# Norm weights as 8 rows spread by TensorE, and the first block's products in another order

## The chip, the cores and the metric

The program runs on one core of one Trainium2 chip. The core has five engines that run their own instruction streams and wait for each other by semaphores: TensorE (in the profile PE, with its weight loads as PEld), VectorE (DVE), ScalarE (ACT), GpSimd (POOL) and SyncE (SP), which here only starts transfers; 16 DMA engines move data between device memory (DRAM), the on-chip buffer and, through the engines, the accumulators (PSUM). The time is the device time of one execution in microseconds (us). Before the change it was 972.03 us, the median of three runs (970.86 to 972.68).

## The reference

One layer of an inference step for a streaming encoder, on 1024 new prompt rows and 64 sample rows of 1024 features, all in f32. What matters here is the beginning:

```python
def rms_norm(x, w):
    xf = x.astype(jnp.float32)
    ms = jnp.mean(xf * xf, axis=-1, keepdims=True)
    return (xf * lax.rsqrt(ms + EPS)).astype(x.dtype) * w

h = rms_norm(x, norm_w) @ w_in          # x: 1088 rows x 1024, w_in: 1024 x 6144
sb_q, sb_k, sb_v, sb_z, cb_q, cb_k, cb_v, cb_z, g_sb, g_cb = jnp.split(h, SPLIT_POINTS, axis=-1)
...                                     # stick-breaking attention, chunk-band attention, gates,
...                                     # two projections, a merge, w_out and the residual
```

So every row is scaled by its own rsqrt and every feature by `norm_w` before any product with `w_in` can be formed.

## The kernel before

The order of the instructions on every engine is the order in which the code emits them (there is no scheduler); each engine works its list off in that order, and the tiles' buffers bring the waits.

**Split products.** Every f32 operand is taken apart into a rounded high part and the rest: `whi` is `wraw` rounded (ScalarE), `wlo` is `wraw` less `whi` (line 124); for the second 512 rows of the weights the tiles are called `wrawx`, `whix`, `wlox`. The same is done to the normed rows: `xa` and `xm` hold the high part of features 0 to 511 and 512 to 1023, `xm` (another half of that tile) and `xb` the low part. A product is then the sum of three: high by high, low by high, high by low, each a matmul with 128 rows as the stationary operand and 256 columns of `w_in` moving.

**Row tiles and blocks.** The 1088 rows are 9 tiles: the sample's 64 rows are tile 8 and come first, then tiles 0 to 7 of 128 rows (`TO = [8] + list(range(8))`). `w_in` is taken in blocks; the first eight (`nb = 8`) have 256 columns each and are the loop `for i in range(nb)`, with the nine tiles inside. A tile takes 24 products (8 slices of 128 features, 3 products each); tile 8 takes 16, since its high and low parts lie side by side in `xs`.

**Preparing a tile** goes along with block 0 and has three steps. `prep_s(t)`: ScalarE squares and sums the tile's rows (`sq`, line 261), GpSimd makes `rs`, the inverse root (lines 251 and 252). `prep_a(t)`: VectorE forms `xn`, the rows by `rs` by `nw`, in two halves (line 269). `prep_b(t)`: TensorE transposes `xn` in two times four pieces into PSUM (`pt`, line 280), ScalarE rounds each half out of it (`xs` line 283, `xa` and `xm` line 288), VectorE subtracts for the low part (lines 284 and 289). `nw` is `norm_w` on all 128 partitions, one transfer of 128 x 1024 values on SP's queue, second behind the sample's rows:

```python
load_x(8)
nw = p1.tile([128, D], F32, name="nw", bufs=1)
SP.dma_start(nw, norm_w[0:1, :].to_broadcast([128, D]))
load_x(0)
load_nat(0, 0)
load_nat(0, 1)
```

`W.split((0, 0), V)` and `W.split((0, 1))` take the first block's weights apart: `whi`, then `wlo` on VectorE, `whix`, then `wlox` on GpSimd. In block 0 the transposes of a tile stand a whole tile ahead of its products: those of tile 0 inside tile 8's products, those of tile 1 behind tile 8, those of tile t+2 behind tile t. Finished tiles are copied out of PSUM by `evac_nat` (`fl`, `vst`, lines 295 to 312) and stored by SP.

After the eight blocks come column units of another form, then both attentions with the remaining products laid among them, the two projections and the output product. TensorE's work in all of these is named in the profile by its line (673, 842, 948, 990, 1097, 1150, 1189, 1509).

Of the kernel before, what the change touches and what calls it, by code (L numbers as in the profile page):

```python
# [32 lines left out]
def hybrid_step_kernel(ctx: ExitStack, tc: tile.TileContext, x_prompt, x_sample, c_sbk, c_sbv, c_cbk, c_cbv,  # L33
# [109 lines left out]
    def xk(s, k):  # L143
        return xhl[s][k // 4][:, k % 4]
# [56 lines left out]
    with ExitStack() as ph:  # L201
# [13 lines left out]
        def load_x(t):  # L215
            xt = p1.tile([128, D], F32, name="xt", bufs=4)
            SP.dma_start(xt[:rows(t)], tok(x_prompt, x_sample, t))
            xts[t] = xt
# [4 lines left out]
                   [128, 4, 256], "" if h == 0 else "x")  # L223

        load_x(8)
        nw = p1.tile([128, D], F32, name="nw", bufs=1)
        SP.dma_start(nw, norm_w[0:1, :].to_broadcast([128, D]))
        load_x(0)
        load_nat(0, 0)
        load_nat(0, 1)  # L230
# [25 lines left out]
        def prep_s(t):  # L256
            r = rows(t)
            sq = p1.tile([128, D], F32, name="sq", bufs=1)
            ms = p1.tile([128, 1], F32, name="ms", bufs=4)
            rst[t] = p1.tile([128, 1], F32, name="rs", bufs=4)  # L260
            A.activation(sq[:r], xts[t][:r], AF.Square, accum_out=ms[:r])
            rsqrt(rst[t][:r], ms[:r], 1.0 / D, 1)

        def prep_a(t):
            r = rows(t)
            xt = xts.pop(t)
            xn = p1.tile([128, D], F32, name="xn", bufs=2)
            for c in (slice(0, 512), slice(512, D)):
                V.scalar_tensor_tensor(xn[:r, c], xt[:r, c], rst[t][:r], nw[:r, c], op0=OP.mult, op1=OP.mult)
            xns[t] = xn  # L270
# [169 lines left out]
                load_raw(2 * i + 4)  # L440

        load_x(3)
        prep_s(8)
        prep_a(8)
        prep_s(0)
        prep_b(8)
        prep_a(0)
        W.split((0, 0), V)
        W.split((0, 1))
        prep_s(1)  # L450
        load_x(4)
        pend, raw1 = [], None
        for i in range(nb):
            for ti, t in enumerate(TO):
                r = rows(t)
                last = (i, ti) >= (nb - 1, NT - 3)
                ps = (psA if ti % 3 == 2 and not last else psF).tile([128, 512], F32, name="acc")[:, :256]
                ns = 2 if t == 8 else 3
                steps = [(k, n) for k in range(KT) for n in range(ns)]
                if i == 0 and ti < 2:  # L460
                    steps.sort(key=lambda e: (e[1], e[0]))
                for m, (k, n) in enumerate(steps):
                    if i == 0 and ti == 0 and m == 4:
                        prep_b(0)
                    w = W.sp[i, k // 4][n // (ns - 1)][:, k % 4]
                    x = xs[:, k] if t == 8 else xk(n % 2, k)[:, xc(t):xc(t) + r]
                    TE.matmul(ps, x, w, start=m == 0, stop=m == len(steps) - 1)  # L467
                if i == 0 and ti == 0:
                    prep_a(1)
                    prep_s(2)  # L470
                    load_x(5)
                if len(pend) >= 3 or (pend and pend[0][0] < i and ti > 3):
                    post_nat(*pend.pop(0))
                if i == 0 and ti + 2 < NT:
                    if ti + 3 < NT:
                        prep_a(TO[ti + 3])
                    prep_b(TO[ti + 2])
                    if ti + 7 < NT:
                        load_x(TO[ti + 7])
                    if ti + 4 < NT:  # L480
                        prep_s(TO[ti + 4])
                got = evac_nat(i, t, ps)
                if raw1:
                    norm_nat(*raw1)
                    pend.append(raw1[:3])
                raw1 = (i, t) + got if got else None
                if i == 0:
                    if ti == 2:
                        load_nat(1, 0)
                        load_nat(1, 1)  # L490
                        SP.dma_start(wqk[:, 0], q_norm_w[0:1, :].to_broadcast([128, 64]))
                        SP.dma_start(wqk[:, 1], k_norm_w[0:1, :].to_broadcast([128, 64]))
                if ti in (3, 6) and i > 0 or ti in (5, 6) and i == 0:
                    h = 1 if ti == 6 else 0
                    if i + 1 < nb:
                        W.split((i + 1, h))
                    if i + 2 < nb:
                        load_nat(i + 2, h)
                    elif h == 0:
                        load_raw(i + 2 - nb)  # L500
                if (i, ti) == (4, 2):
                    load_rb()
                if 0 <= 9 * i + ti - 40 < 8:
                    make_rb(9 * i + ti - 40)
                if i >= 5 and p1x is not None and not pend and not raw1 and ti >= 3:
                    p1x.close()
                    p1x = None
                    tp = sx.enter_context(tc.tile_pool(name="tp", bufs=1))
                    pad(tp, 64)
                    tms = [[tp.tile([128, 4, HF], F32R, name=f"t{n}{s}") for s in "hl"] for n in range(4)]  # L510
                    ws = sx.enter_context(tc.tile_pool(name="ws", bufs=3))
                    tq = ph.enter_context(tc.tile_pool(name="tq", bufs=3))
                    tjobs = iter(make_t(tms, tq))
                    tw = [3]
                if p1x is None:
                    tw[0] -= 1
                    if tw[0] < 0:
                        next(tjobs, None)
                if (i, ti) == (nb - 1, 5):
                    prep(0)  # L520
                if (i, ti) == (nb - 1, 6):
                    presum(1)
                if (i, ti) == (nb - 1, 7):
                    prep(1)
                if (i, ti) in ((0, 4), (2, 3)):
                    cache_load("sb" if i == 0 else "cb")
                at = {(1, 1): 0, (1, 4): 1, (1, 7): 2, (2, 1): 3}
                if (i, ti) in at:
                    cache_pair("sb", at[i, ti])
                if (i - 2, ti) in at:  # L530
                    cache_pair("cb", at[i - 2, ti])
                if (i, ti) in ((1, 1), (1, 5)):
                    for s in range(2):
                        h = ti // 4
                        for c in range(2):
                            o = 512 + c * HF
                            G.tensor_copy(xhl[s][h][:, :, o:o + 32],
                                          xs[:, 4 * h:4 * h + 4, 64 * s + 32 * c:64 * s + 32 * c + 32])
                if (i, ti) == (1, 0):
                    V.tensor_scalar(wqk[:, 0], wqk[:, 0], -0.125, None, op0=OP.mult)  # L540
# [1054 lines left out]
```

## Time and profile before

| what | value |
|---|---|
| median of 3 runs | 972.03 us |
| profiled execution, its own time | 971.06 us |
| its span, first to last instruction | 969.3 us |
| HBM read and written | 112.94 MB and 62.00 MB |
| SP's queue (q1) | 159.98 MB, 56.2% of 16 DMA engines |
| ScalarE's queue (q10) | 8.33 MB, 2.7% |
| loads of `xt` from the prompt, 512 KB each | 5.2 us from issue to landing (median of 8) |
| loads of `wraw` from `w_in`, 512 KB each | 4.4 us (median of 31) |

A line of the timeline reads: start and duration in us, engine, line of the code, operation, what is written from what, shape, and in brackets how long the engine sat idle before it and who ended that. In a line of groups the busy time, the mean in ns and the idle time stand behind the count. In a row of stretches the limits come first, then the length, then busy time and instructions of PE, PEld, DVE, ACT and POOL, the clock, the share of the DMA engines and GB/s. A busy TensorE need not be a fast one: a matmul's duration is modelled and overlaps the next, so the pace is read from weight loads and from the distance between starts.

### The profile page before, as it was taken

How to read it: one execution, taken by the hardware profiler on the slowest of the kernel's cores; microseconds unless marked ns; L12 is line 12 of the kernel's file. 1: busy time of each engine (PE TensorE's matmuls, PEld its weight loads, DVE VectorE, ACT ScalarE, POOL GpSimd, SP SyncE). 2: the span in 40 equal slices, each digit the busy share in tenths (PEclk: the TensorE clock that was granted, in tenths of full speed). 3: DMA queues.
4: the chain of work that ended last, by engine and by line, in shares of the span. 5: the costliest groups of instructions: out<-in, count | busy, mean ns of one | idle time of the engine just before them, and what ended most of it. 6: DMA issues, size and time to landing. Idle time of an engine off the chain costs nothing.

```text
span 969.3 us, 20419 instructions
## 1 busy us (share of the span) xinstructions
PE 951.8 (98%) x7604; PEld 906.1 (93%) x7604; DVE 587.9 (61%) x1166; ACT 475.5 (49%) x1056; POOL 393.6 (41%) x391
## 2 busy tenths in 40 slices
PE   6999999999999999999999999999999999999998
PEld 5999999999999999999999987777888988999998
DVE  5456665696454555543332298776777865499735
ACT  6544443344444343333332377667886874465220
POOL 3276664215454566655542200011331111586641
PEclk9999999999999999999999999999999999999999
DMA  7727567534646565555533997769799832862742
GB/s 243 226 84 244 196 223 253 177 93 133 183 138 191 182 182 176 154 178 168 164 96 92 271 251 216 181 173 246 226 292 255 245 105 82 260 193 70 221 133 78
DMA packets 173512, 176.28 MB, mean 182 GB/s; under 512 B 30753, under 2 KB 157597, under 8 KB 173286
## 3 DMA queue, kind: packets, MB, share of 16 engines
q1 hardware_dynamic: 161878, 159.98, 56.2%
q10 hardware_dynamic: 8720, 8.33, 2.7%
q0 software_dynamic: 2816, 6.69, 2.2%
q8 instruction: 60, 0.98, 0.5%
q14 instruction: 38, 0.31, 0.1%
HBM read 112.94 MB, written 62.00 MB: 180 GB/s over the span
## 4 chain that ended last, share of the span: by engine, by line
PE 95%; ACT 1%; DMA 1%; SPq 1%; issue 0%; POOL 0%; DVE 0%; ACTq 0%; DVEq 0%
PE b L673 30%; PE acc L467 20%; PE b L1509 8%; PE z L1097 7%; PE o L1189 7%; PE pt L1150 7%; PE b L990 5%; PE acc L842 5%; PE acc L948 4%; PE pk L352 1%; DMA wrawx<-in_w_in_dram 1%; PE pt L280 1%; PE acc L1545 1%; DMA ot<-d_ocb 0%; PE acc L598 0%
## 5 line engine op out<-in xcount | busy, mean ns | idle before, releaser
L1150 PE MATMUL pt<-ident,be 128*128 128x128 f32 (+1 forms) x568 | 87.7, 278 | 1.9 <-ACT wT L1159 1.6
L1097 PE MATMUL z<-ks,sq 128*128 128x320 f32 (+5 forms) x384 | 88.3, 338 | 0.0
L1119 DVE TENSOR_TENSOR_SCAN be<-be,imp 128x128 f32<-128x128 f32 (+7 forms) x64 | 83.2, 1340 | 7.6 <-ACT be L1100 7.6
L1150 PEld LDWEIGHTS pt<-ident,be 128*128 128x128 f32 (+1 forms) x568 | 66.3, 140 | 15.2 <-issue 4.6
L1159 ACT ACTIVATE wT<-pt 128x512 f32<-128x512 f32 (+3 forms) x125 | 58.1, 500 | 44.6 <-PE pt L1150 44.5
L467 PE MATMUL acc<-whi,xa 128*128 128x256 f32 x256 | 74.2, 292 | 0.0
L467 PE MATMUL acc<-wlox,xm 128*128 128x256 f32 x256 | 70.7, 278 | 0.0
L467 PE MATMUL acc<-whi,xm 128*128 128x256 f32 x256 | 70.7, 278 | 0.0
L467 PE MATMUL acc<-wlo,xa 128*128 128x256 f32 x256 | 70.7, 278 | 0.0
L467 PE MATMUL acc<-whix,xb 128*128 128x256 f32 x256 | 70.6, 278 | 0.0
L467 PE MATMUL acc<-whix,xm 128*128 128x256 f32 x256 | 70.6, 278 | 0.0
L681 DVE TENSOR_TENSOR u<-b,s 128x256 f32<-128x256 f32 (+1 forms) x56 | 24.2, 439 | 73.2 <-PE b L673 72.1
L1097 PEld LDWEIGHTS z<-ks,sq 128*128 128x128 f32 x384 | 63.9, 190 | 2.0 <-ACT be L1100 0.9
L1189 PE MATMUL o<-wT,vp 128*64 128x256 f32 (+1 forms) x608 | 64.2, 356 | 0.0
L1189 PEld LDWEIGHTS o<-wT,vp 128*64 128x64 f32 x608 | 40.3, 136 | 23.6 <-issue 6.6
L1122 ACT ACTIVATE be<-be,sm 128x640 f32<-128x640 f32 (+5 forms) x68 | 47.3, 695 | 17.0 <-DVE sm L1121 17.0
L124 POOL TENSOR_TENSOR wlo<-wraw,whi 128x1024 fp32r<-128x1024 f32 x15 | 36.4, 2427 | 46.7 <-ACT whi L117 43.2
L746 POOL DMA_DIRECT2D d_osb<-zt x20 | 10.8, 540 | 104.5 <-DVE zt L1198 72.2
L1100 ACT ACTIVATE be<-z 128x384 f32<-128x384 f32 (+6 forms) x104 | 48.1, 519 | 4.5 <-PE z L1097 3.9
L437 POOL TENSOR_TENSOR whix<-ws,whix 128x512 fp32r<-128x512 f32 x28 | 36.9, 1317 | 31.6 <-ACT whix L436 31.6
L1110 ACT ACTIVATE be<-be,sm 128x640 f32<-128x640 f32 (+5 forms) x68 | 47.3, 696 | 4.7 <-DVE sm L1102 4.3
L467 PEld LDWEIGHTS acc<-whi,xa 128*128 128x128 f32 x256 | 47.9, 188 | 0.1
(306 smaller groups left out, 3184.3 us busy)
## 6 DMA issues: line engine op xcount, KB each, us to landing
wraw<-in_w_in_dram SPq DMA_DIRECT2D x31, 512.0 KB, 4.4
wrawx<-in_w_in_dram SPq DMA_DIRECT2D x17, 512.0 KB, 4.5
sq<-d_qsbT SPq DMA_DIRECT2D x32, 192.0 KB, 4.2
sq<-d_qcbT SPq DMA_DIRECT2D x32, 192.0 KB, 5.3
xt<-in_x_prompt_dram SPq DMA_DIRECT2D x8, 512.0 KB, 5.2
d_kcbT<-hl SPq DMA_DIRECT2D x8, 512.0 KB, 4.4
d_qcbT<-hl SPq DMA_DIRECT2D x8, 512.0 KB, 3.1
d_ksbT<-hl SPq DMA_DIRECT2D x16, 256.0 KB, 2.8
```

The lines of the kernel that those rows point to most:

```text
L467: TE.matmul(ps, x, w, start=m == 0, stop=m == len(steps) - 1)
L673: TE.matmul(ps[:, :m], w[:, hl_, k], right[s](x)[:, k, a:b], start=s < 3 and k == 0 and e == 0, stop=k == 3 and e == 2, skip_group_check=s ...
L842: TE.matmul(ps[:, :b - a], w[:, k], xk(x, k)[:, a:b], start=k == 0 and n == 0, stop=k == KT - 1 and n == 2)
L990: TE.matmul(pp[uu][:, :n], w[:, p, uu * 128:uu * 128 + 128], g[:, a:e], start=p == 0 and m == 0, stop=p == NPAIR - 1 and m == 2)
L1097: TE.matmul(z[:, :m], s[:, e, q0:q0 + 128], ks[:, h, o + x:o + y], start=(e, h) == parts[0], stop=(e, h) == parts[-1])
L1100: A.activation(be[:r, x:y], z[:r, :m], AF.Sigmoid, scale=-0.125)
L1110: A.activation(be[:, :n], be[:, :n], AF.Exp, bias=kp[:, j:j + 1], scale=-1.0, accum_out=kp[:, 2:3])
L1119: V.tensor_tensor_scan(be[:r, n - 1::-1], be[:r, n - 1::-1], im[:, ::-1], 0.0, op0=OP.mult, op1=OP.max)
L1150: TE.transpose(pt[:kr, x, :r], be[:r, kb * 128:kb * 128 + kr], ident[:r, :r])
L1159: A.activation(w[:, sl:sl + m, q0:q0 + r], pt[:, :m, :r], AF.Copy)
L1189: TE.matmul(o[hd * 64:hd * 64 + 64, c0:c1], vv[:kr, kb, hd * 64:hd * 64 + 64], wT[b, p, j, hd, s // 4][:kr, s % 4, c0:c1] if j < 4 else wT ...
L1509: TE.matmul(ps[:, t], left[s](xs_, k)[:, ts_], wt_[:, k], start=s < 3 and t == k == e == 0, stop=k == 3 and e == 2, skip_group_check=s > 2 ...
```

## The change

**The norm weights.** The 128 x 1024 transfer on SP is gone. In its place ScalarE's queue loads `norm_w` as 8 rows of 128 values (`nw8`). TensorE transposes it to 128 x 8 (`nwt`, copied out by VectorE). Then each of the 8 columns, repeated 128 times by its access pattern, is transposed, which puts that column's 128 values on every partition; VectorE copies the two halves out of PSUM (`spread`, two of the `acc` buffers) into `nw`. Around these stand `beat(n)`: n matmuls of the identity by itself, whose result (`idle`) nobody reads: 4 ahead, 1 behind the first transpose, 3 behind the spread, 5 behind the transposes of tile 8.

**The first block's parts.** Both `whi` come before both `wlo`; `wlox` of block 0 moves from GpSimd to VectorE.

**Transposes among products.** In block 0 the products of every tile are ordered by part. The transposes of tile j+1 come inside tile j's products, first behind 20 of the 24, then 16, 12, 8, 4, 0 (`ready`); `ready(j)` also emits `xn` of tile j+1, `sq` of tile j+2 and the load of tile j+5. Tile 8's last four products (`part8`) stand inside tile 0's, and its copy out of PSUM comes behind tile 0's products.

TensorE before, from the start of the program to the second half of tile 8 (`whi` by `xs` are tile 8's products):

```order
L280 MATMUL pt<-ident,xn 128x64 x8
L467 MATMUL acc<-whi,xs 128x256 x4
L280 MATMUL pt<-ident,xn 128x128 x8
L467 MATMUL acc<-whix,xs 128x256 x4
L467 MATMUL acc<-wlo,xs 128x256 x4
L467 MATMUL acc<-wlox,xs 128x256 x4
```

The same place now (`nw_176` is the tile `nw8`, `pc` is `idle`):

```order
L447 MATMUL pc<-ident 128x128 x4
L452 MATMUL acc<-ident,nw_176 128x8
L447 MATMUL pc<-ident 128x128
L458 MATMUL acc<-ident,nwt 128x128 x8
L447 MATMUL pc<-ident 128x128 x3
L280 MATMUL pt<-ident,xn 128x64 x8
L447 MATMUL pc<-ident 128x128 x5
L490 MATMUL acc<-whi,xs 128x256 x4
```

Nine transposes and 13 beats now stand around tile 8's transposes, ahead of the first product.

TensorE before, from the transposes of tile 1 to those of tile 2, with tile 0's products between:

```order
L280 MATMUL pt<-ident,xn 128x128 x8
L467 MATMUL acc<-whi,xa 128x256 x4
L467 MATMUL acc<-whix,xm 128x256 x4
L467 MATMUL acc<-whi,xm 128x256 x4
L467 MATMUL acc<-whix,xb 128x256 x4
L467 MATMUL acc<-wlo,xa 128x256 x4
L467 MATMUL acc<-wlox,xm 128x256 x4
L280 MATMUL pt<-ident,xn 128x128 x8
```

The same now, from the first products of tile 0:

```order
L490 MATMUL acc<-whi,xa 128x256 x4
L490 MATMUL acc<-whix,xm 128x256 x4
L490 MATMUL acc<-wlox,xs 128x256 x4
L490 MATMUL acc<-whi,xm 128x256 x4
L490 MATMUL acc<-whix,xb 128x256 x4
L490 MATMUL acc<-wlo,xa 128x256 x4
L280 MATMUL pt<-ident,xn 128x128 x8
L490 MATMUL acc<-wlox,xm 128x256 x4
```

The transposes of tile 1 went from ahead of tile 0 to behind 20 of its 24 products, and tile 8's last four came into it.

VectorE before, from the start to the first `xn` of tiles 1 and 2:

```order
L269 SCALAR_TENSOR_TENSOR xn<-xt,rs,nw 64x512 x2
L284 TENSOR_TENSOR xs<-pt,xs 128x4x64 x2
L269 SCALAR_TENSOR_TENSOR xn<-xt,rs,nw 128x512 x2
L124 TENSOR_TENSOR wlo<-wraw,whi 128x1024
L289 TENSOR_TENSOR xm<-pt,xa 128x4x128
L289 TENSOR_TENSOR xb<-pt,xm 128x4x128
L269 SCALAR_TENSOR_TENSOR xn<-xt,rs,nw 128x512 x4
```

And now:

```order
L453 COPY nwt<-acc 128x8
L460 COPY nw<-acc 128x512 x2
L269 SCALAR_TENSOR_TENSOR xn<-xt,rs,nw 64x512 x2
L284 TENSOR_TENSOR xs<-pt,xs 128x4x64 x2
L269 SCALAR_TENSOR_TENSOR xn<-xt,rs,nw 128x512 x2
L124 TENSOR_TENSOR wlo<-wraw,whi 128x1024
L124 TENSOR_TENSOR wlox<-wrawx,whix 128x1024
L289 TENSOR_TENSOR xm<-pt,xa 128x4x128
L289 TENSOR_TENSOR xb<-pt,xm 128x4x128
L269 SCALAR_TENSOR_TENSOR xn<-xt,rs,nw 128x512 x4
```

Three copies came ahead of the first `xn`, and `wlox` between `wlo` and the low part of tile 0.

```diff
--- before.py
+++ after.py
@@ -223,8 +223,8 @@
                    [128, 4, 256], "" if h == 0 else "x")
 
         load_x(8)
-        nw = p1.tile([128, D], F32, name="nw", bufs=1)
-        SP.dma_start(nw, norm_w[0:1, :].to_broadcast([128, D]))
+        nw8 = pn.tile([8, 128], F32, name="nw8", bufs=1)
+        A.dma_start(nw8, norm_w[0:1, :].rearrange("o (k n) -> (o k) n", n=128))
         load_x(0)
         load_nat(0, 0)
         load_nat(0, 1)
@@ -440,16 +440,54 @@
                 load_raw(2 * i + 4)
 
         load_x(3)
+        idle = psK.tile([128, 4, 128], F32, name="pc")
+
+        def beat(n):
+            for k in range(n):
+                TE.matmul(idle[:, k % 4], ident, ident, start=True, stop=True)
+
+        beat(4)
+        nwt = pn.tile([128, 8], F32, name="nwt", bufs=1)
+        spread = [psF.tile([128, 512], F32, name="acc") for c in range(2)]
+        TE.transpose(spread[0][:, 0:8], nw8, ident[:8, :8])
+        V.tensor_copy(nwt, spread[0][:, 0:8])
+        beat(1)
+        nw = p1.tile([128, D], F32, name="nw", bufs=1)
+        for c in range(2):
+            for k in range(4):
+                TE.transpose(spread[c][:, k * 128:(k + 1) * 128],
+                             nwt[:, 4 * c + k:4 * c + k + 1].to_broadcast([128, 128]), ident)
+            V.tensor_copy(nw[:, c * 512:(c + 1) * 512], spread[c])
+        beat(3)
         prep_s(8)
         prep_a(8)
         prep_s(0)
         prep_b(8)
+        beat(5)
         prep_a(0)
-        W.split((0, 0), V)
-        W.split((0, 1))
-        prep_s(1)
+        W.hi((0, 0))
+        W.hi((0, 1))
+        W.lo((0, 0), V)
+        W.lo((0, 1), V)
         load_x(4)
         pend, raw1 = [], None
+
+        def ready(j):
+            if 0 < j < 7:
+                prep_a(j + 1)
+            prep_b(j)
+            if j == 0:
+                prep_s(1)
+                prep_a(1)
+            if j + 2 < 8:
+                prep_s(j + 2)
+            if j + 5 < 8:
+                load_x(j + 5)
+
+        def product(ps, t, ns, k, n, first, last):
+            w = W.sp[i, k // 4][n // (ns - 1)][:, k % 4]
+            x = xs[:, k] if t == 8 else xk(n % 2, k)[:, xc(t):xc(t) + rows(t)]
+            TE.matmul(ps, x, w, start=first, stop=last)
         for i in range(nb):
             for ti, t in enumerate(TO):
                 r = rows(t)
@@ -457,28 +495,24 @@
                 ps = (psA if ti % 3 == 2 and not last else psF).tile([128, 512], F32, name="acc")[:, :256]
                 ns = 2 if t == 8 else 3
                 steps = [(k, n) for k in range(KT) for n in range(ns)]
-                if i == 0 and ti < 2:
+                if i == 0:
                     steps.sort(key=lambda e: (e[1], e[0]))
+                    if ti == 0:
+                        part8, steps = steps[12:], steps[:12]
                 for m, (k, n) in enumerate(steps):
-                    if i == 0 and ti == 0 and m == 4:
-                        prep_b(0)
-                    w = W.sp[i, k // 4][n // (ns - 1)][:, k % 4]
-                    x = xs[:, k] if t == 8 else xk(n % 2, k)[:, xc(t):xc(t) + r]
-                    TE.matmul(ps, x, w, start=m == 0, stop=m == len(steps) - 1)
+                    if i == 0 and m == (4, 20, 16, 12, 8, 4, 0, 0, -1)[ti]:
+                        ready(ti)
+                    if i == 0 and ti == 1 and m == 8:
+                        for m8, e in enumerate(part8):
+                            product(ps8, 8, 2, *e, False, m8 == 3)
+                    product(ps, t, ns, k, n, m == 0, ti + i > 0 and m == len(steps) - 1)
                 if i == 0 and ti == 0:
-                    prep_a(1)
-                    prep_s(2)
-                    load_x(5)
+                    ps8 = ps
+                    continue
+                if i == 0 and ti == 1:
+                    evac_nat(0, 8, ps8)
                 if len(pend) >= 3 or (pend and pend[0][0] < i and ti > 3):
                     post_nat(*pend.pop(0))
-                if i == 0 and ti + 2 < NT:
-                    if ti + 3 < NT:
-                        prep_a(TO[ti + 3])
-                    prep_b(TO[ti + 2])
-                    if ti + 7 < NT:
-                        load_x(TO[ti + 7])
-                    if ti + 4 < NT:
-                        prep_s(TO[ti + 4])
                 got = evac_nat(i, t, ps)
                 if raw1:
                     norm_nat(*raw1)
```

## The prediction

> **What bounds the kernel now.** I read the page's shares first, then the stretches, the waits of TensorE, and last the start, instruction by instruction.
>
> ```profile
> span 969.3 us, 20419 instructions
> PE 951.8 (98%) x7604; PEld 906.1 (93%) x7604; DVE 587.9 (61%) x1166; ACT 475.5 (49%) x1056; POOL 393.6 (41%) x391
> PEclk9999999999999999999999999999999999999999
> PE 95%; ACT 1%; DMA 1%; SPq 1%; issue 0%; POOL 0%; DVE 0%; ACTq 0%; DVEq 0%
> ```
>
> TensorE is the bound: 98% busy, 95% of the chain that ended last. So an edit counts by how far it moves TensorE's stream of work, and the stretches say where that stream has holes.
>
> ```profile
> 0.00:17.36 17.36, 7.85 (x40) 7.03 (x41) 7.41 (x12) 9.81 (x16) 7.75 (x16) 1.00 0.72 257
> 17.36:45.00 27.64, 27.64 (x243) 27.64 (x242) 17.19 (x27) 17.23 (x35) 8.46 (x12) 1.00 0.69 217
> 45.00:950.00 905.00, 901.15 (x7195) 856.57 (x7195) 552.42 (x1113) 448.12 (x1005) 374.95 (x362) 1.00 0.62 181
> PE acc L948 <- DVE xm L952: 1.4, 1, 1.4
> ```
>
> The first two figures of a row are its length and TensorE's busy time. Until 17.36 TensorE works 7.85 us; from there to 45.00 it has no hole, and of the 3.85 us missing up to 950.00 the longest wait (last row) is 1.4 us. Whatever TensorE gains before about 24 us therefore reaches the end, as long as the stream stays closed. The start itself:
>
> ```profile
> 0.75 0.59 SPq L217 DMA_DIRECT2D xt<-in_x_sample_dram  x1
> 1.03 0.29 POOL masks.py:199 TENSOR_SCALAR_AFFINE_SELECT ident<-ident 128x128 f32<-128x128 f32 x1
> 4.51 1.06 ACT L261 ACTIVATE sq<-xt 64x1024 f32<-64x1024 f32 x1 [2.48 <-DMA xt<-in_x_sample_dram]
> 6.02 0.58 POOL L252 TENSOR_TENSOR rs<-rs,half 64x1 f32<-64x1 f32 x1
> 6.63 1.41 DVE L269 SCALAR_TENSOR_TENSOR xn<-xt,rs,nw 64x512 f32<-64x512 f32 x2 [6.63 <-POOL rs L252]
> 7.42 1.06 ACT L261 ACTIVATE sq<-xt 128x1024 f32<-128x1024 f32 x1 [1.75 <-DMA xt<-in_x_prompt_dram]
> 7.43 1.35 PE L280 MATMUL pt<-ident,xn 64*128 64x64 f32 x8 [7.43 <-DVE xn L269]
> 8.59 0.66 ACT L283 ACTIVATE xs<-pt 128x256 fp32r<-128x256 f32 x2
> 9.00 0.76 DVE L284 TENSOR_TENSOR xs<-pt,xs 128x256 fp32r<-128x256 f32 x2 [0.97 <-ACT xs L283]
> 9.13 1.06 ACT L117 ACTIVATE whi<-wraw 128x1024 fp32r<-128x1024 f32 x1
> 9.68 1.41 DVE L269 SCALAR_TENSOR_TENSOR xn<-xt,rs,nw 128x512 f32<-128x512 f32 x2
> 10.24 0.93 PEld L467 LDWEIGHTS acc<-whi,xs 128*128 128x128 f32 x4 [1.65 <-ACT whi L117]
> 11.00 1.22 DVE L124 TENSOR_TENSOR wlo<-wraw,whi 128x1024 fp32r<-128x1024 f32 x1
> 11.12 1.66 PEld L280 LDWEIGHTS pt<-ident,xn 128*128 128x128 f32 x8
> 11.65 1.06 ACT L261 ACTIVATE sq<-xt 128x1024 f32<-128x1024 f32 x1 [0.28 <-DMA xt<-in_x_prompt_dram]
> 12.71 0.58 ACT L288 ACTIVATE xa<-pt 128x512 fp32r<-128x512 f32 x1
> 13.32 0.69 DVE L289 TENSOR_TENSOR xm<-pt,xa 128x512 fp32r<-128x512 f32 x1 [1.10 <-ACT xa L288]
> 13.93 0.68 DVE L289 TENSOR_TENSOR xb<-pt,xm 128x512 fp32r<-128x512 f32 x1
> 14.51 0.93 PEld L467 LDWEIGHTS acc<-wlox,xs 128*128 128x128 f32 x4
> 16.28 0.42 PEld L280 LDWEIGHTS pt<-ident,xn 128*128 128x128 f32 x4 [0.84 <-issue]
> 17.33 0.54 PEld L467 LDWEIGHTS acc<-whi,xa 128*128 128x128 f32 x4
> 23.88 0.90 PEld L280 LDWEIGHTS pt<-ident,xn 128*128 128x128 f32 x8
> ```
>
> ```profile
> 2.95 7.34 DMA wrawx<-in_w_in_dram
> 10.31 1.07 ACT whix L117
> 11.45 3.00 POOL wlox L124
> 14.81 0.58 POOL rs L252
> 15.41 0.76 DVE xn L269
> 17.61 2.83 PE acc L467 x24
> 20.44 0.87 PE pt L280 x8
> ```
>
> The second fence is the chain through the start: second weight half lands (10.29), ScalarE rounds it, GpSimd subtracts for 3.00 us, and only behind that does GpSimd serve rs of tile 1, so xn(1) begins at 15.41. From 17.33 on a tile costs 2.83 for 24 products and 0.87 for 8 transposes.
>
> The weight loads show a second thing. Four products take 0.93 at 14.51 and 0.54 at 17.33; eight transposes take 1.66 at 11.12 and 0.90 at 23.88. Until somewhere in 15.44 to 16.28 TensorE runs at half speed, though PEclk reads full throughout, so that view does not hold this. The speed doubled 5.2 to 6.0 us after TensorE became continuously busy (10.24), behind a hole of some 1.5 us.
>
> **The change, part by part.** The mark I compare is the start of the transposes of tile 3, 23.88 before: up to there both programs have given TensorE the same products and transposes, the spread and the beats apart, and behind it the same work is left.
>
> *The 512 KB broadcast leaves SP's queue.* From x(0) landed (7.42) to wrawx landed (10.29) two loads of 512 KB took 2.87, 1.43 each; x(1) came 1.36 later. Without norm_w ahead, all of these come 1.43 earlier: x(0) at 5.97, wrawx at 8.86, x(1) at 10.2. The sample's rows stand ahead of norm_w and stay at 4.51, so rs of tile 8 stays at 6.60 and xn(8) at 6.63.
>
> *The small load and the spread.* Eight rows go out on ScalarE's queue at about 0.7. No such load is in the trace; the sample's 256 KB, issued at 0.75, landed by 4.51, which bounds it above, and I take 3.2. Then one transpose, a small copy, eight transposes (0.2 each at half speed) and two copies from PSUM, each like this one:
>
> ```profile
> 813.34 0.69 DVE L1161 COPY wT<-pt 128x512 f32<-128x512 f32 x1 [0.15 <-PE pt L1150]
> ```
>
> 3.2 + 0.3 + 0.3 + 0.9 + 0.7 puts the first half of nw at 5.4, the second at about 6.3: ahead of 6.63, so it costs nothing while rs(8) covers it; a landing at 4.5 would cost about 1.0.
>
> *The beats.* A beat (plain f32, 128x128 by the identity) has no row. Lower end: a transpose through the same identity, 0.11 at full and 0.21 at half speed. Upper end: 0.46, a half-speed product that nothing overlaps:
>
> ```profile
> L467 PE MATMUL acc<-whi,xs 128*128 128x256 f32 x4 | 1.2, 457 | 1.5 <-ACT whi L117 1.5
> ```
>
> Four, one and three beats lie in holes. The five behind the transposes of tile 8 (they end at 8.78) fit before 10.2 unless they cost more than 0.28 each; at 0.46 they push the first products 0.9 back. I take 0.18 at full speed and twice that cold: this kernel spends three rounded products of 0.118 where one f32 product would do, and a beat has half their width. [...]
>
> *wlox on VectorE, sq and xn reordered.* The second half of xs follows the transposes (8.78) and ends at 9.15 on ScalarE; whi behind it stays at 9.13; whix moves 0.12 forward (10.19, ready 11.26). VectorE: xs done 9.55, xn(0) to 10.96, wlo (1.22) to 12.2, wlox (1.22 instead of GpSimd's 3.00) to 13.4, against 14.45 before. Behind it wait xm and xb of tile 0, which end at 14.1 and 14.7 (they follow each other by 0.61). ScalarE: xa, xm of tile 0 from 11.3, sq(1) at 12.3; from sq to rs takes 2.09 (4.51 to 6.60), so rs(1) comes at 14.4, no longer behind the subtract. Then xn(1) 14.7 to 16.1, xn(2) to 17.5, xm(1) to 18.2, xb(1) to 18.8.
>
> *TensorE's order, at full speed* (0.47 for four products, 0.87 for eight transposes): whi·xs 10.2 to 10.7; transposes of tile 0 to 11.5; whix·xs to 12.0; wlo·xs waits for wlo, to 12.7; eight of tile 0 to 13.6; wlox·xs to 14.1; xm and xb each wait for VectorE, to 15.2; wlo·xa to 15.7; transposes of tile 1 to 16.5; four more to 17.0. Tile 1: eight to 18.0, xm(1) waits to 18.2 and ends 18.7, xb(1) ends 19.3, transposes of tile 2 to 20.1, eight products to 21.1. From xb(1) on TensorE has no wait.
>
> The mark falls at 21.0 to 21.1 instead of 23.88: **2.85 us gained**. After it the period is 3.70 a tile. VectorE and ScalarE were each busy 17.2 of the 27.64 of that stretch, 2.3 of each 3.70, so the shorter lead of the transposes should hold.
>
> **The sum.** Profiled execution 971.06 (span 969.3 and 1.8 around it): 966.4 + 1.8 = 968.2. The median of the three runs is 0.97 above it, so on that level 972.03 - 2.85 = 969.2.
>
> **The clock.** All of this supposes full speed by about 10. The row for it: 5.2 to 6.0 us after continuous work began. With beats from 1.4 (the identity is ready at 1.32) and only short holes behind them that gives 6.6 to 7.4, and 3 us are to spare.
>
> **Rivals.**
>
> *A hole resets the clock.* Between the last beat of the spread (6.1 to 6.9) and xn(8) TensorE waits 0.5 to 1.3. Before, 1.5 us of idling did not let the earlier transposes count. If it is so again, full speed comes 6.0 after 7.43, at 13.4. Then cold beats end at 9.8 to 11.1, the first products and the transposes of tile 0 (1.66) at 12.8 to 13.5, and the mark at 21.7 to 22.3: gain 1.6 to 2.2, about 970.1.
>
> *Transposes do not fill the clock's account.* Then the beats alone, 8 in 7.4 us, are too thin, and the run of products is broken by the cold transposes of tile 0. With full speed at 15.8 as before, the same walk from the beats' end gives 23.1 to 23.7, at 17.3 0.7 more: between 0.8 gained and 0.5 lost, about 971.8. For it: before, the speed came after nearly 3 us of unbroken products. Against it: that stretch too followed transposes without a hole. [...]
>
> *The small load comes late (slower).* The whole of VectorE's chain hangs on nw. Landing behind the large loads on the shared engines, it costs 1 us for each us past 3.5; from 6.4 on the gain is gone, and at 8.7 (the bias loads' median, 7.4 us, behind an issue that ends at 1.3) the kernel takes 972.03 + 5.2 - 2.85 = 974.4.
>
> ```profile
> bias<-d_rb SPq DMA_DIRECT2D x8, 320.0 KB, 7.4
> ```
>
> Against it: the sample's 64 times larger load landed by 4.51.
>
> **How the numbers follow.** Forecast 0.60, reset 0.12, no count 0.16, late load 0.12. The likeliest gives 969.2, with 968.3 to 970.2 as its own range (runs differ by 0.9 either way). The range reaches from 967.9 up to 972.3, taking in the reset and most of the no-count case. 0.2% is 1.94 us, about what a measurement of this kernel can tell from no change. Faster by more: 0.56 of the forecast and half of the reset, 0.62. Within: 0.04, 0.06, 0.11 and 0.02, 0.23. Slower: 0.05 and 0.10, 0.15.
>
> **What would show it.** Right: weight loads near 0.12 for products by 10.5, wlox on VectorE ending near 13.4, xn(1) near 14.7, the transposes of tile 3 near 21.0, the second block's first product near 42.2 and no wait of TensorE between 19 and 42. Wrong: products at 0.23 beyond 13, xn(8) later than 6.7, or holes at the moved transposes.

## The result, and the profile after

The changed kernel took 968.82 us, the median of seven executions (968.42 to 970.13), against 972.33 (970.86 to 974.33, seven) for the kernel before on the same chip. The ratio is 0.9966, with a 95% interval of 0.9956 to 0.9976: some 3.3 us faster by the ratio (the medians lie 3.5 apart). The prediction had 969.2 and called a gain over 0.2% the likeliest outcome.

The single execution that was profiled needs a word, since it is one of the two long ones (970.03; the seven fall into five between 968.42 and 968.97 and two near 970.1). Its shares and stretches, in the columns of the prediction's own rows:

```profile
span 968.3 us, 20492 instructions
PE 957.8 (99%) x7639; PEld 912.0 (94%) x7639; DVE 593.5 (61%) x1170; ACT 476.6 (49%) x1056; POOL 392.8 (41%) x390
...
0.00:17.36 17.36, 14.38 (x93) 13.48 (x94) 9.92 (x15) 9.68 (x16) 4.91 (x15) 0.90 0.68 227
17.36:45.00 27.64, 27.31 (x237) 27.05 (x237) 17.47 (x27) 18.10 (x36) 8.83 (x13) 1.00 0.79 242
```

TensorE is busy for 14.38 us of the first 17.36 instead of 7.85, but part of that is beats, and the clock column of that stretch reads 0.90: some of it ran at half speed. The start of this execution, instruction by instruction:

```profile
1.37 1.78 PEld L447 LDWEIGHTS pc<-ident 128*128 128x128 f32 x8 [1.37 <-POOL half L234]
3.38 0.18 PEld L452 LDWEIGHTS acc<-ident,nw 8*128 8x128 f32 x1 [0.23 <-issue]
5.17 1.29 DVE L460 COPY nw<-acc 128x512 f32<-128x512 f32 x2 [1.32 <-PE acc L458]
5.30 0.75 PEld L447 LDWEIGHTS pc<-ident 128*128 128x128 f32 x6
6.06 1.06 ACT L261 ACTIVATE sq<-xt 128x1024 f32<-128x1024 f32 x1 [0.22 <-DMA xt<-in_x_prompt_dram]
6.82 1.41 DVE L269 SCALAR_TENSOR_TENSOR xn<-xt,rs,nw 64x512 f32<-64x512 f32 x2 [0.35 <-POOL rs L252]
7.61 0.32 PEld L280 LDWEIGHTS pt<-ident,xn 64*128 64x128 f32 x4 [1.56 <-DVE xn L269]
8.88 2.21 PEld L447 LDWEIGHTS pc<-ident 128*128 128x128 f32 x10
10.97 0.90 PEld L490 LDWEIGHTS acc<-whi,xs 128*128 128x128 f32 x4
22.45 0.54 PEld L490 LDWEIGHTS acc<-whi,xa 128*128 128x128 f32 x4
```

A beat shows as two records, so x8 is four beats, x6 three, x10 five. The loads have moved as planned: x(0) at 6.06, and the eight rows are there by 3.38. The four first beats are cold, 0.44 each; the three at 5.30 take 0.25 each, so TensorE already has full speed there. Then it waits 1.56 us before the transposes of tile 8, and the five beats at 8.88 are cold again, 0.44 each. The rows by the microsecond show that this time the profile's clock column records it (third figure from the end):

```profile
8.00:9.00 1.00, 0.80 (x7) 0.61 (x5) 0.65 (x2) 0.39 (x2) 0.66 (x1) 0.66 1.07 393
9.00:10.00 1.00, 1.00 (x5) 1.00 (x6) 0.59 (x2) 1.00 (x2) 0.00 (x0) 0.50 1.01 401
11.00:12.00 1.00, 1.00 (x7) 1.00 (x7) 1.00 (x2) 0.27 (x1) 0.00 (x0) 0.63 0.95 381
12.00:13.00 1.00, 1.00 (x11) 1.00 (x10) 1.00 (x2) 0.45 (x1) 0.00 (x0) 1.00 0.79 213
```

The prediction's mark, the point up to which both programs have done the same products and transposes, is the last row of the start: 22.45, against 23.88 before, so 1.43 gained in this execution. (Before, this point is the start of tile 3's transposes; in the new order it is the first product of tile 2, `whi` by `xa`, and the transposes of tile 3 come 12 products later.) Of that 1.0 arrives at the end (span 968.3 against 969.3). Two rows name where the difference went and came from. On the chain, one run of 488 products of the blocks takes 1.1 longer; and the one long wait of TensorE late in the kernel is 0.9 shorter (1.4 before):

```profile
169.45 56.42 PE acc L490 x488
...
PE acc L982 <- DVE xm L986: 0.5, 1, 0.5
```

The kernel before has `170.37 55.33 PE acc L467 x488` in the first row's place. These two nearly cancel; the remaining 0.2 lies in nothing that I could name. The first of them is no accident of this execution, as the version with the broadcast will show. In all profiles of this study the time from the mark to the end of the span is 944.1 to 946.1, so a mark is worth its difference to within about 1 us either way.

### The profile page after: what moved, and what is told of

The parts are those of the page before. It is cut to its first block, busy times and chain, and to the rows that moved or that the text cites. A ratio compares the mean times of both kernels' runs of the same rounds, so it can differ in the third digit from the quotient of the medians.

```text
span 968.3 us, 20492 instructions
## 1 busy us (share of the span) xinstructions
PE 957.8 (99%) x7639; PEld 912.0 (94%) x7639; DVE 593.5 (61%) x1170; ACT 476.6 (49%) x1056; POOL 392.8 (41%) x390
## 4 chain that ended last, share of the span: by engine, by line
PE 96%; ACT 1%; DVE 1%; DMA 1%; issue 0%; POOL 0%; ACTq 0%; DVEq 0%; POOLq 0%
PE b L707 30%; PE acc L490 20%; PE b L1543 8%; PE o L1223 7%; PE z L1131 7%; PE pt L1184 7%; PE b L1024 5%; PE acc L876 5%; PE acc L982 5%; PE pk L352 1%; PE pt L280 1%; PE acc L1579 1%; PE acc L632 0%; DMA xt<-in_x_sample_dram 0%; PE pc L374 0%; ACT wT L1193 0%
## 5 line engine op out<-in xcount | busy, mean ns | idle before, releaser
L490 PE MATMUL acc<-whi,xa 128*128 128x256 f32 x256 | 70.5, 291 | 0.0
L490 PE MATMUL acc<-whi,xm 128*128 128x256 f32 x256 | 67.6, 279 | 0.3 <-DVE xm L289 0.3
L490 PE MATMUL acc<-wlox,xm 128*128 128x256 f32 x256 | 67.5, 279 | 0.0
L490 PE MATMUL acc<-whix,xb 128*128 128x256 f32 x256 | 67.5, 279 | 0.0
L490 PE MATMUL acc<-whix,xm 128*128 128x256 f32 x256 | 67.5, 279 | 0.0
L490 PE MATMUL acc<-wlo,xa 128*128 128x256 f32 x256 | 67.4, 279 | 0.0
L1156 ACT ACTIVATE be<-be,sm 128x640 f32<-128x640 f32 (+5 forms) x68 | 47.4, 697 | 16.7 <-DVE sm L1155 16.6
L490 PEld LDWEIGHTS acc<-whi,xm 128*128 128x128 f32 x256 | 46.4, 188 | 0.5 <-DVE xm L289 0.5
```

The source lines that it names most:

```text
L490: TE.matmul(ps, x, w, start=first, stop=last)
```

## The experiments

Each run below gives the median of its executions, their range and number, and the ratio to the kernel before on the same chip. In the same three sessions the kernel before had medians of 972.25, 972.19 and 971.68. "Theory C" in the expectations is the prediction's own: the gain is the fast clock and the new order together. The "equal-work mark" is the mark above.

**The changed kernel once more, and the kernel before once more.** No edit, to see how one execution differs from the next.

> The changed kernel once more beside the others of this call. Theory C: 968.4 to 970.2 with a median near 968.9, the slow executions those with a mean granted clock of 0.998; in the new profile either the clock holds (mark 21.0 to 21.3) or it falls back in the hole ahead of the transposes of tile 8 (mark near 22.4).

> The kernel before once more, for its profile alone. [...]

The changed kernel: 969.93 (968.29 to 970.73, 11), ratio 0.9973 [0.9964, 0.9983]. The profiled execution (968.47, span 966.7) is one of the short ones, and its clock reads 1.00 throughout:

```profile
5.66 1.40 PEld L447 LDWEIGHTS pc<-ident 128*128 128x128 f32 x6
7.51 0.33 PEld L280 LDWEIGHTS pt<-ident,xn 64*128 64x128 f32 x4 [0.45 <-DVE xn L269]
8.57 1.19 PEld L447 LDWEIGHTS pc<-ident 128*128 128x128 f32 x10
10.05 0.53 PEld L490 LDWEIGHTS acc<-whi,xs 128*128 128x128 f32 x4 [0.30 <-ACT whi L117]
13.44 0.55 PEld L490 LDWEIGHTS acc<-wlox,xs 128*128 128x128 f32 x4
16.22 1.41 DVE L269 SCALAR_TENSOR_TENSOR xn<-xt,rs,nw 128x512 f32<-128x512 f32 x2 [0.45 <-POOL rs L252]
18.29 0.54 PEld L490 LDWEIGHTS acc<-whi,xm 128*128 128x128 f32 x4 [0.52 <-DVE xm L289]
19.36 0.90 PEld L280 LDWEIGHTS pt<-ident,xn 128*128 128x128 f32 x8
21.17 0.54 PEld L490 LDWEIGHTS acc<-whi,xa 128*128 128x128 f32 x4
```

The five beats at 8.57 take 0.24 each, the first products run at full speed at 10.05, and the mark is at 21.17. The three beats at 5.66 still run at half speed here, so full speed comes only between 7.06 and 7.51, where the first profile had it by 5.30. That makes the hole ahead of tile 8's transposes shorter: the slow beats end at 7.06 instead of 6.05, which leaves 0.45 instead of 1.56. So here an early release lengthened the very hole in which the clock then fell. The other group of this kernel's executions, five of 968.3 to 968.9 and six of 969.9 to 970.7, has the clock at 1.0 in nearly all of its members (one is at 0.998). So the fall seen in the first profile explains that execution, not all of the longer ones. The half speed at the very start is not recorded as a lower clock (before, TensorE works at half pace from 10 to 16 with PEclk at full), so a late first release would leave no sign in the summary of an execution that was not profiled. That stays open; in the profiles with beats it is nowhere later than 7.5.

The kernel before took 971.53 in its one execution (span 969.7, mark 24.37):

```profile
15.00 0.93 PEld L467 LDWEIGHTS acc<-wlox,xs 128*128 128x128 f32 x4
16.77 0.42 PEld L280 LDWEIGHTS pt<-ident,xn 128*128 128x128 f32 x4 [0.84 <-issue]
24.37 0.90 PEld L280 LDWEIGHTS pt<-ident,xn 128*128 128x128 f32 x8
```

Full speed comes between 15.9 and 16.8, 5.2 to 6.0 us behind the first products (10.73), as in the first profile (10.24), so these two show no scatter; the profiles with beats do. Between these two profiles the mark differs by 3.2 and the span by 3.0.

**The change without the beats.** The order, the parts on VectorE, the small load and the spread stay.

```diff
         def beat(n):
-            for k in range(n):
+            for k in range(0):
```

> The changed kernel without any beat. Theory C (the gain is the clock and the new order together): the clock stays at half speed until about 15, the equal-work mark (end of tile 1's products and of the transposes of tile 2, 23.88 before) falls at 23.0 to 23.7, so 0.2 to 0.9 us are left of the gain, 971.4 to 972.1 beside 972.3. Rival O (the order and wlox on VectorE do it, the beats are idle work) and rival L (the 512 KB taken off SP's queue does it): 968.8, or less, since five beats no longer stand ahead of the first product.

971.72 (970.71 to 972.71, 11), ratio 0.9996 [0.9987, 1.0006]: nothing is left of the gain. The mark is at 22.96, 0.9 ahead of the kernel before, but the span of 969.1 is only 0.2 shorter; where the rest goes is seen in the version with the broadcast.

```profile
10.58 0.93 PEld L490 LDWEIGHTS acc<-whi,xs 128*128 128x128 f32 x4 [1.60 <-ACT whi L117]
11.45 1.66 PEld L280 LDWEIGHTS pt<-ident,xn 128*128 128x128 f32 x8
13.09 0.89 PEld L490 LDWEIGHTS acc<-whix,xs 128*128 128x128 f32 x4
13.92 0.55 PEld L490 LDWEIGHTS acc<-wlo,xs 128*128 128x128 f32 x4
22.96 0.54 PEld L490 LDWEIGHTS acc<-whi,xa 128*128 128x128 f32 x4
```

In this execution the clock is released 3.3 us after the products begin at 10.58, and half of those 3.3 us are transposes.

**The beats without the order.** The kernel before, with the same number of beats.

```diff
         load_x(3)
+        idle = psK.tile([128, 4, 128], F32, name="pc")
+        (beat as in the changed kernel)
+        beat(15)
         prep_s(8)
...
         prep_b(8)
+        beat(5)
```

> The kernel before with 15 beats at the start and 5 behind the transposes of tile 8, nothing else. Theory C: no gain, 971.9 to 972.5: the products of tile 8 run at full speed but the transposes of tile 1 still wait for xn(1), which waits behind wlox on GpSimd until 15.4; only the wait grows. If the clock alone is the gain: 969.

971.68 (970.06 to 974.62, 12), ratio 0.9998 [0.9985, 1.0012]: nothing either.

```profile
12.00 3.00 POOL L124 TENSOR_TENSOR wlox<-wrawx,whix 128x1024 fp32r<-128x1024 f32 x1 [1.95 <-ACT whix L117]
15.05 0.53 PEld L475 LDWEIGHTS acc<-wlox,xs 128*128 128x128 f32 x4 [1.70 <-POOL wlox L124]
15.96 1.42 DVE L269 SCALAR_TENSOR_TENSOR xn<-xt,rs,nw 128x512 f32<-128x512 f32 x2 [0.80 <-POOL rs L252]
16.83 1.57 PEld L280 LDWEIGHTS pt<-ident,xn 128*128 128x128 f32 x8 [1.25 <-issue]
18.38 0.98 PEld L475 LDWEIGHTS acc<-whi,xa 128*128 128x128 f32 x4
```

TensorE, now fast, only arrives earlier at the same waits: 1.70 for wlox from GpSimd, then for xn(1), which VectorE begins at 15.96 whatever TensorE does. Behind these holes the clock falls (eight transposes in 1.57, four products in 0.98; the clock column has 0.50 from 16.6 to 20.0), and the profiled mark is 25.67, later than before. The four executions in which the clock reads 0.999 or 1.0 take 970.06 to 970.16, the eight with 0.996 to 0.998 take 970.7 to 974.6. So part of what the median hides is the falls; as the kernel before, run beside it, also has executions down to 970.15, what beats alone would be worth without falls is not shown.

**More beats in the hole in front of tile 8.**

```diff
-        beat(3)
+        beat(6)
```

> The changed kernel with 6 beats instead of 3 behind the spread, so that TensorE's hole ahead of the transposes of tile 8 shrinks from 1.4 to about 0.8 us. Theory C: the hole no longer lets the clock fall back, the executions near 970.1 go, all lie at 968.4 to 969, mean granted clock 1.0 in each, mark near 21.1. If the two groups have another cause: still about two in seven near 970.1.

969.2 (968.58 to 971.34, 11), ratio 0.9974 [0.9963, 0.9985]; mark 21.17, span 967.0, and the clock holds from the transposes of tile 8 on. But executions of 970.42, 970.6 and 971.34 remain, with clocks of 0.999 to 1.0, so the longer group did not go, though that had been expected.

**The broadcast back.** `norm_w` again as one load of 128 x 1024 on SP's queue, no rows, no spread; beats and order as in the changed kernel.

```diff
-        nw8 = pn.tile([8, 128], F32, name="nw8", bufs=1)
-        A.dma_start(nw8, norm_w[0:1, :].rearrange("o (k n) -> (o k) n", n=128))
+        nw = p1.tile([128, D], F32, name="nw", bufs=1)
+        SP.dma_start(nw, norm_w[0:1, :].to_broadcast([128, D]))
...
-        beat(4)
-        (nwt, the nine transposes and three copies of the spread, beat(1), beat(3))
+        beat(15)
```

> The changed kernel with the 128 x 1024 norm_w transfer back on SP's queue and 15 beats in the place of the 8 rows and the spread. Theory C: 969.0 to 969.4, since from 9 on VectorE's chain hangs on the sample's rows and not on x(0) or wrawx, so 1.4 us later loads cost only 0.1 to 0.3. Rival L: 971.5 or more.

> The kernel with the broadcast and 15 beats once more. If it is really ahead of the changed kernel: 967.4 to 968.4 again. If the first reading was a lucky one: 968.8 or more.

967.9 (967.36 to 969.12, 5), ratio 0.996 [0.9945, 0.9975], and in another session 968.39 (967.54 to 969.22, 5), ratio 0.9963 [0.9951, 0.9976]. The marks are 21.83 and 22.49, spans 967.3 and 966.6.

```profile
7.90 1.06 ACT L261 ACTIVATE sq<-xt 128x1024 f32<-128x1024 f32 x1 [1.95 <-DMA xt<-in_x_prompt_dram]
8.76 1.19 PEld L447 LDWEIGHTS pc<-ident 128*128 128x128 f32 x10
10.72 0.53 PEld L478 LDWEIGHTS acc<-whi,xs 128*128 128x128 f32 x4 [0.77 <-ACT whi L117]
21.83 0.54 PEld L478 LDWEIGHTS acc<-whi,xa 128*128 128x128 f32 x4
```

x(0) comes 1.47 later than in the changed kernel's second profile (7.90 against 6.43). ScalarE has `sq` of tile 0 ahead of `xs` and `whi`, so the late rows reach the first products, 0.67 later (10.72 against 10.05), and the mark, 0.66 later (21.83 against 21.17). In the second profile with the broadcast x(0) comes at 8.55, the first products at 11.38 and the mark, at 22.49, is 1.32 later. From the first products to the mark all three take 11.1. The expectation of 0.1 to 0.3 was too small.

Yet the total is not longer: both medians lie below those of the changed kernel (968.82 and 969.93), with intervals that overlap. The stretch of 488 products shows part of the reason; first the changed kernel's second profile, then the second one with the broadcast:

```profile
168.34 56.43 PE acc L490 x488
169.08 55.33 PE acc L478 x488
```

All four profiles of versions with the small load and the spread have 56.42 or 56.43 here, all nine without them, those of the kernel before among them, have 55.33. From the mark to the end of this stretch the four take 203.4 to 203.6 us and the nine 201.7 to 201.9. So the small load and the spread gain 0.7 to 1.3 by the mark and lose some 1.7 behind it. Later stages make up for part of that, and in the total the two ways can't be told apart for certain; but every median of a version with the broadcast, the beats and the new order (967.9 to 968.59) lies below every median with the spread, the beats and the new order (968.82 to 969.93). Why the same products run slower in the versions with the spread was not tried.

**wlox back on GpSimd**, in the version with the broadcast.

```diff
-        W.lo((0, 1), V)
+        W.lo((0, 1))
```

> The kernel with the broadcast and the 15 beats (967.9 us), with wlox of block 0 back on GpSimd. Theory C with the prediction's walk: wlox ends about 1.1 later than on VectorE (3.00 instead of 1.22 behind whix), TensorE stands 0.7 to 0.8 ahead of wlox by xs, rs(1) comes behind wlox and xn(1) 0.7 later; the equal-work mark moves from 21.8 to about 22.6, 968.6 to 968.9. Rival (VectorE is the bound of the start, so taking 1.22 off it gains): 967.0 to 967.5.

968.34 (968.11 to 969.68, 5), ratio 0.9962 [0.9948, 0.9975]. The start behaves as expected, the total not:

```profile
14.83 0.53 PEld L478 LDWEIGHTS acc<-wlox,xs 128*128 128x128 f32 x4 [0.78 <-POOL wlox L124]
```

The wait for wlox is 0.78, and from the first products (10.55) to the mark (22.55) it takes 12.0 instead of 11.1. But the median is 0.4 above the first one with wlox on VectorE and level with the second (968.39). Once the order has put other products ahead of wlox, taking the subtract off GpSimd is worth 0.9 at the mark and nothing that these medians can show.

**Beats and the parts on ScalarE and VectorE, with the old order of the products.** From the version with beats alone:

```diff
-        W.split((0, 0), V)
-        W.split((0, 1))
+        W.hi((0, 0))
+        W.hi((0, 1))
+        W.lo((0, 0), V)
+        W.lo((0, 1), V)
```

> The kernel before with 15 and 5 beats, both whi ahead of both wlo, and wlox on VectorE, but the old order of products and transposes in block 0. Theory C: rs(1) is free at about 14.1, the transposes of tile 1 still stand ahead of tile 0's products and wait for xn(1) until about 15.9; mark about 23.4, 970.5 to 971.7, and the hole ahead of them (1.5 us) lets the clock fall back in some executions. Rival (wlox on VectorE is the gain, the order only follows): 968 to 969.

970.39 (968.71 to 972.24, 12), ratio 0.9976 [0.9965, 0.9988]; mark 23.57, span 969.2.

```profile
15.98 0.42 PEld L280 LDWEIGHTS pt<-ident,xn 128*128 128x128 f32 x4 [1.48 <-issue]
23.57 0.90 PEld L280 LDWEIGHTS pt<-ident,xn 128*128 128x128 f32 x8
```

Its executions stand in two groups: 968.7 to 969.0 where the clock reads 0.999 or 1.0 (the profiled one, 971.02, is the exception), and 970.05 to 972.24 where it reads 0.997 or 0.998. The hole of 1.48 in front of tile 1's transposes is what the new order removes. In the profiled execution the clock holds through it; that it falls there in others is read only from their lower clock. Against the version with the broadcast, which differs only in the order, the mark is 1.1 to 1.7 later (23.57 against 22.49 and 21.83), and from the first products (10.79) to the mark it takes 12.8 instead of 11.1. By the medians, beats and the parts on VectorE bring a good half of the gain (0.9976, between 0.9998 for beats alone and 0.996 with the order too), and the order the rest, though the intervals of that last step overlap a little. Some of the rest comes by the wait that the order removes, some by the executions in which the clock does not fall; these two I can't separate.

**Transposes for beats.** The version with the broadcast, each beat replaced by two transposes of the identity.

```diff
-            for k in range(n):
-                TE.matmul(idle[:, k % 4], ident, ident, start=True, stop=True)
+            for k in range(2 * n):
+                TE.transpose(idle[:, k % 4], ident, ident)
```

> The kernel with the broadcast, with each beat replaced by two transposes of the identity: 30 at the start and 10 behind the transposes of tile 8. If transposes release the clock as products do: full speed between 4.8 and 8.2, first products at full pace, 967.5 to 968.5 as with beats. If they do not count (the rule of the no-count rival): half speed until 14 or later, 971 to 972 as without any beat.

968.08 (967.33 to 968.46, 5), ratio 0.9958 [0.9944, 0.9971], mark 21.81, span 966.7:

```profile
1.37 5.21 PEld L447 LDWEIGHTS pc<-ident 128*128 128x128 f32 x30 [1.37 <-POOL half L234]
10.69 0.54 PEld L478 LDWEIGHTS acc<-whi,xs 128*128 128x128 f32 x4 [1.06 <-ACT whi L117]
```

Ahead of the first product TensorE has done nothing but transposes, and that product runs at full pace (0.54 for four). Transposes release the clock here as products do.

**The five beats behind tile 8's transposes taken out**, in the version with the broadcast.

```diff
         prep_b(8)
-        beat(5)
```

> The kernel with the broadcast and the 15 beats at the start, without the five behind the transposes of tile 8. A hole of about 2 us then stands between those transposes and the first products. Theory C: the clock falls back in most executions, for up to 3.4 us, 0.5 to 1.7 us lost: 968.5 to 969.6, slow executions with a mean granted clock of 0.998. If a hole of 2 us is harmless: 967.9.

968.59 (967.89 to 969.66, 5), ratio 0.9966 [0.9953, 0.9978]. All five executions have the clock at 0.996 to 0.998, and the profile shows why (stretches first, then the start):

```profile
9.00:10.00 1.00, 0.00 (x0) 0.00 (x0) 0.68 (x3) 1.00 (x3) 0.73 (x2) 0.69 1.14 393
...
15.00:16.00 1.00, 1.00 (x6) 1.00 (x6) 0.00 (x0) 0.97 (x3) 0.67 (x2) 0.50 0.03 12
16.00:17.00 1.00, 1.00 (x10) 1.00 (x9) 0.88 (x2) 0.34 (x2) 0.59 (x2) 0.89 0.00 0
```

```profile
10.56 0.93 PEld L477 LDWEIGHTS acc<-whi,xs 128*128 128x128 f32 x4 [2.17 <-ACT whi L117]
11.43 1.66 PEld L280 LDWEIGHTS pt<-ident,xn 128*128 128x128 f32 x8
23.39 0.53 PEld L477 LDWEIGHTS acc<-whi,xa 128*128 128x128 f32 x4
```

A hole of 2.17 us makes the clock fall at about 9.4, and it comes back at about 16.2, 6.8 us later. Half pace lasts over four products (0.93) and eight transposes (1.66) and more. The mark is 0.9 to 1.6 later than with the five beats (23.39 against 22.49, 21.83 and, with transposes for beats, 21.81), and from the first products to the mark it takes 12.8 instead of 11.1. Yet the medians differ by 0.2 to 0.7, within the intervals: part of what the start loses is not lost at the end, and where it is regained I did not find.

## Why the prediction came out right

**The mechanism: confirmed.** The forecast was that fast clock and new order together move TensorE's stream 2.85 us ahead. Beats alone give 0.9998, the change without beats 0.9996, both together 0.9966 and 0.9973. Without the spread it is 0.996 and 0.9963, with wlox left on GpSimd as well 0.9962, so neither of these two is needed for it. The gain is an interaction, as the walk through TensorE's list had it: without the beats the products run cold up to 13.92, without the order TensorE waits for wlox and xn(1).

**The walk: confirmed where the clock holds.** The mark was put at 21.0 to 21.1 and is at 21.17 in the second profile; its span, put at 966.4, is 966.7. First products: put at 10.2, at 10.05. wlox·xs: to begin at 13.6, at 13.44. The wait for xm(1): put at 18.2, at 18.29. Transposes of tile 2: from 19.3, at 19.36. The second block's first product, put at 42.2, came at 42.44 there and at 43.54 in the first profile (45.04 before). One sign was misnamed: "the transposes of tile 3 near 21.0" is the old name of the mark; in the new order these transposes come at 22.60.

**Part of the agreement is luck.** Within the start, xn(1) begins at 14.36 (put at 14.7), but xn(2) then waits 0.45 for GpSimd's `rs`, a wait that the walk did not have, and begins at 16.22 (put at 16.1): the two errors nearly cancel in xm(1). Behind the mark the prediction had "the same work is left". By work that is so, by time not: up to the end of the 488 products the changed kernel takes 1.8 us longer in its second profile than the kernel before in its first, and about as much comes back later, 1.2 of it in the one long wait of TensorE (0.2 instead of 1.4). Only so does the gain at the mark, 2.7, reach the span as 2.6.

**The reset by a hole: a rival with too small a chance.** It had 0.12 and the mark at 21.7 to 22.3. The first profile is that case: a hole of 1.56 us, five beats cold, mark 22.45, just past that range. The prediction held it unlikely beside a forecast without it; the runs show that both occur in executions of the same program, so they should have been a mixture within the forecast. What it costs here, 1.28 in the mark and 1.6 in the execution (970.03 against 968.47), was about the size worked out. Its expected return of speed "6.0 after 7.43, at 13.4" was too late: it came at about 11.7.

**The time to release: taken as fixed, and it varies.** The prediction took 5.2 to 6.0 us from the trace of the kernel before. That holds in both profiles of that kernel, and the second profile of the changed one is close to it: the beats begin at 1.37 and full speed comes between 7.06 and 7.51, 5.7 to 6.1 later. But it is 3.3 without beats (10.58 to 13.92) and at most 3.9 in the first profile (1.37 to 5.30). In the six profiles in which 15 beats stand in a row, these take 4.88 to 6.24 us; at 0.44 cold and 0.24 warm that puts the release 2.8 to 5.8 us behind the first beat, as an estimate. Where the clock falls later, it stays low for 3.4 us in two profiles (8.3 to 11.7 in the first one, 16.6 to 20.0 with beats alone) and for 6.8 in the version without the five. Holes of 1.56 us, in the first profile of the changed kernel, and of 2.17, in the version without the five, were enough for the clock to fall; in the profiled execution with the old order holes of 1.56 (6.30 to 7.86) and 1.48 were not. With 3 us to spare this variation cost the forecast nothing.

**Transposes do not count: refuted.** It had 0.16. Without beats they fill half of the 3.3 us to release, and by themselves they release the clock (0.54 for the first four products).

**The beats: mis-sized, harmless in the forecast's case.** Put at 0.36 cold and 0.18 warm, they take 0.44 and 0.24 to 0.25, each as two records. For a cold one the upper end, 0.46, was nearer. Warm, five end 0.3 ahead of the first products; cold, they push them back to 10.97, as the prediction's upper end (0.9 back) had warned.

**The small load: in time, a gain at the mark, and a loss behind it.** The rows are there by 3.38 (put at 3.2; without beats TensorE has them at 2.25 already), and both halves of nw by 6.46 to 6.81 (put at 6.3). xn(8) begins at 6.82 and 6.73 instead of 6.63: the first time because the sample's rows came later (4.69 instead of 4.51), the second behind the copy of the second half. The rival of a late landing did not occur. The step that the loads come 1.43 earlier is about right (x(0) 6.06 and 6.43 against a forecast of 5.97), but it is worth only 0.7 to 1.3 in the mark, as the broadcast shows, and nothing that the total shows: the versions with it are some 1.7 slower behind the mark. The prediction had listed it as a step of the sum without asking what the sum would be without it.

**The level.** 2.85 was taken off the median of three runs, 972.03. The measured medians lie 3.5 and 2.3 apart, 3.3 and 2.6 by the two ratios (0.9966 of 972.33; 0.9973 of 972.19), around that figure, with groups of executions 1.5 us apart in the changed kernel. This scatter, not the walk, limits how closely such a forecast can come.

## What to carry to other kernels

Here a filled clock and a better order were each worth nothing that could be measured alone (0.9998 and 0.9996) and some three microseconds together (0.9966 and 0.9973): before dropping an edit that "does nothing", look at what its engine waits for next. Filling idle time on TensorE paid only with the waits behind it shortened, and filling has to reach across the last hole too: holes of 1.56 and 2.17 us undid, in two profiles, what all beats before them had bought, and transposes did as filler as well as beats (968.08 against 967.9 and 968.39). Try each part of a bundle on its own: here the part with the most code, the spread of the norm weights, could be left out, and the simpler version measured 967.9 to 968.4. And follow a gain past the point where it is made: the spread's lead at the mark was lost again within the next 200 us.

## What the runs showed of the hardware unexpectedly

TensorE's half speed shows in the clock column of these profiles only when it follows a fall: before, the products at half pace in the first 16 us stand under a clock of 1.00 as the row of the kernel before has it (six weight loads where the changed kernel's row for 12 to 13 has ten):

```profile
13.00:14.00 1.00, 1.00 (x6) 1.00 (x6) 0.68 (x2) 1.00 (x3) 1.00 (x1) 1.00 1.05 418
```

In the version without the five beats and in the first profile of the changed one the same pace stands under 0.50. So here the clock column can't be trusted for the first microseconds; the duration of weight loads can (four take 0.93 at half pace and 0.54 at full).

And at full clock the distance between products is not constant. In the first profiles of both kernels it changes, in bouts, between some 113.3 and 117.7 ns. In the stretch of 488 products quoted above the changed kernel has two bouts of some 14 us at the longer distance (177 to 190 and 201 to 215), and the kernel before has none. What this costs follows the version, not the execution: 56.42 or 56.43 in all four profiles with the spread, 55.33 in all nine without it, 1.1 us, a third of what this change gains, from an edit that does not touch these products. The cause was not tried.
